# A fused encoder layer on one core: other layouts for two stores in DRAM, row maxima spread evenly over the projection, and the scheduler's detailed model of the chip

## The chip, the core and the metric

The kernel runs on one core of one Trainium2 chip, as one program and one launch. The metric is device time in microseconds (us) from start to end. All arithmetic is float32 in and out; the matrix products use pairs of fp32r numbers, a high half and a low half of each operand, so that one product of two float32 matrices becomes three matmuls (high by high, high by low, low by high).

## What is computed

One layer (DEPTH is 1) on x of 2048 tokens by 1024 features, then a final RMSNorm:

```python
xn = rms_norm(x, mix_norm_g[l])
h = xn @ w_in[l]                                  # 1024 x 2568
q, k, v, f_logit, z = jnp.split(h, [512, 1024, 1536, 1544], axis=-1)
log_f = jax.nn.log_sigmoid(f_logit + b_f[l])
attn = forgetting_attention(q, k, v, log_f)       # 8 heads of 64; logit[t,s] = q.k/8 + c[t] - c[s], s <= t
sgu = spatial_gating(gelu(z), ln_g, ln_b, w_s, b_s)   # z = (zu, zv); zu * (w_s @ layer_norm(zv) + b_s) in chunks of 128
merged = concat([rms_norm(attn, g1), rms_norm(sgu, g2)], axis=-1)
x = x + merged @ w_out[l]                         # 1024 x 1024
xn = rms_norm(x, ffn_norm_g[l])
gate, up = jnp.split(xn @ w_gate_up[l], 2, axis=-1)   # 1024 x 5632
x = x + (silu(gate) * up) @ w_down[l]             # 2816 x 1024
return rms_norm(x, final_norm_g)
```

## The kernel before

**Stage 1, the projections (to about 342 us of the profiled execution).** The tokens stand in four chunks `c` of 512. For each chunk the transposed input is scaled and cut into high and low halves (`xh`, `xl`, four pieces of two k-tiles each, `Chunk.halves`), and TensorE makes q (`which` 0), k (`which` 1) and v. One *unit* of that loop is 24 matmuls into one PSUM tile `mm`: eight k-tiles, three products each. A chunk after the first has 12 units: four for q, four for k, four for v. The halves are also kept in DRAM for a later stage: `Chunk.keep` stores them in `XS`, whose layout is by groups of 128 tokens, [128, 4, 2, 8, 128], so that a later load of one group is one run of 8 KB in each partition, while the store has runs of 128 numbers. v goes to `VD`, laid out by heads, [8, 512, 129].

Between the units stand the row maxima of the chunk before: `max_stream` makes, for each head and block of 128 queries, one matmul into a PSUM tile `mx_ps` and one reduction on VectorE (`one_max`, L357 to L362). `between(n_early, ...)` after each unit takes `n_early` steps of that stream, 3, 6 and 7 in the chunks 1, 2 and 3. Where they stand among the matmuls is settled by the framework's scheduler.

**Stage 2, attention and gating (about 342 to 976 us).** The work is 320 *steps*, each a block of 128 keys against 512 queries of one head. `qk` makes the logits with two matmuls into `mx_ps` (L714, L715), ScalarE takes the exponential (`Pt`, L717) and the high half (`Ph`, L123), VectorE the low half (`Pl`, L126), GpSimd masks blocks on the diagonal (L727), and `pv_of` multiplies with the values, two or three matmuls into `tp` (L747, L749, L752). `mx_ps` has two buffers, which the maxima of stage 2 use too; `Ph` and `Pl` have three. The loop issues the pv of a step two steps behind its qk (DEPTH).

Into these steps the loop mixes the gating branch: `z_proj` makes the z product, 32 tiles of 24 matmuls each (L872, 768 in all), first for zv (tiles of `w` from `wzv`), then for zu. Four tiles make one group of 512 tokens, whose layer norm, gating product (`v_side`, 24 matmuls at L913) or transposes (`u_side`, L940) follow while the next group's product runs. These helpers put their VectorE and ScalarE work behind the newest attention step (`with behind(*newest)`), and share two PSUM buffers `z` with the product. The loop hands out z so that it reaches step 280 (ZEND): 2.4 matmuls a step in the mean. Each z tile needs 1 MB of `XS` (`xz`, two buffers), loaded by GpSimd's queue (L865); the first tile comes from the two halves `wsth` and `wstl`, loaded by SyncE's queue. From about step 281 the output projection (L1127) takes the place of z.

**Stage 3 (to the end).** The rest of the output projection, then the feed-forward part as a seven-product scheme on blocks (L1614, 5544 matmuls).

[...]

Of the kernel before, what the change touches and what calls it, by code (L numbers as in the profile page):

```python
# [16 lines left out]
P = 128  # L17
# [31 lines left out]
HE = [8, 8, 5]  # L49
EB = [1, 12, 12, 10]  # L50

# [34 lines left out]
def trunk(ctx: ExitStack, tc: tile.TileContext, x, x_t, mix_g, w_in, b_f, ln_g, ln_b, w_st, b_st, on_g, w_out,  # L86
# [23 lines left out]
    def behind(*ins):  # L110
# [4 lines left out]
        return s  # L115

    ld = nc.sync.dma_start

    def ldr(o, i):
        return nc.sync.dma_start(f(o), f(i))  # L120
# [27 lines left out]

    XS = [T(dram, [P, 4, 2, KT, P], F32R, f"XS{c}") for c in range(NCH)]
    QH = [[T(dram, [P, CH], F32R, f"QH{p}_{c}") for c in range(NCH)] for p in range(4)]  # L150
    QL = [[T(dram, [P, CH], F32R, f"QL{p}_{c}") for c in range(NCH)] for p in range(4)]
    KH = [[T(dram, [P, CH], F32R, f"KH{p}_{c}") for c in range(NCH)] for p in range(4)]
    KL = [[T(dram, [P, CH], F32R, f"KL{p}_{c}") for c in range(NCH)] for p in range(4)]
    VD = [T(dram, [H, CH, P + 1], F32R, f"VD{c}") for c in range(NCH)]
    FD = [T(dram, [H, CH], F32, f"FD{c}") for c in range(NCH)]
# [85 lines left out]
    class Chunk:  # L241
# [23 lines left out]

        def keep(self, i):
            for a, t in enumerate((self.hi[i], self.lo[i])):
                for m in range(2):
                    s = ldr(XS[self.c][:, :, a, 2 * i + m, :], t[:, m].rearrange("p (t q) -> p t q", t=4))

# [80 lines left out]
    def aug_rows(h, s, r):  # L351
        return AUG.rearrange("(b h) r t -> h r b t", h=H)[h, r, 4 * s : 4 * s + 4, :]

    def one_max(ps, pp, a, j, s, lhs, Dt, mx):
        n = CH if s < j else (a + 1) * P
        pm = T(ps, [P, CH], F32, "mx_ps", **({"bufs": NMX} if ps is ps2_[0] else {}))
        nc.tensor.matmul(pm[:, 0:n], lhs, Dt[0 : lhs.shape[0], 0:n], start=True, stop=True)  # L357
        if s < j:
            nc.vector.tensor_reduce(mx[:, a, s : s + 1], pm, AX.X, ALU.max)  # L359
        else:  # L360
            jk = T(pp, [P, CH], F32, "jk", bufs=1)
            nc.vector.tensor_tensor_reduce(jk[:, 0:n], pm[:, 0:n], dmask[:, CH - n : CH], 1.0, NEG,  # L362
                                           ALU.add, ALU.max, mx[:, a, s : s + 1])
# [62 lines left out]

    def between(n, *done):
        with behind(*done):
            next(gates_, None)
            next(xg, None)  # L430
        for _ in range(n):
            next(early, None)

    def queue(c):
# [14 lines left out]
    def v_close(pm, xc, tt):  # L449
# [7 lines left out]
        b = nc.vector.scalar_tensor_tensor(v[:, :, DH + 1 : P], pmv[:, :, 1:DH], r, f(v[:, :, 1:DH]), ALU.mult, ALU.subtract)  # L457
        s = queue(xc.c if xc.c < NCH - 1 or tt < 2 else 0).dma_start(f(VD[xc.c][:, tt * P : (tt + 1) * P, :].rearrange("h p d -> p h d")), f(v))
        if xc.c == NCH - 1 and tt == 1:
# [58 lines left out]
    for c in range(NCH):  # L518
# [25 lines left out]
        for which, w in ((0, wq), (1, wk)):  # L544
            for pr in range(4):
                pm = T(ps1m, [P, CH], F32, "mm", bufs=4)
                n = 0
                for k in range(KT):
                    lh, ll = w[0][:, k, pr * P : (pr + 1) * P], w[1][:, k, pr * P : (pr + 1) * P]
                    rh, rl = xh[k // 2][:, k % 2, :], xl[k // 2][:, k % 2, :]  # L550
                    for a, b in ((lh, rh), (lh, rl), (ll, rh)):
                        mm = nc.tensor.matmul(pm, a, b, start=n == 0, stop=n == 3 * KT - 1)
                        n += 1
                qh = T(p1, [P, CH], F32R, "qh")
# [22 lines left out]
                if which == (c == 0):  # L577
                    with behind(s):
                        xc.keep(pr)
                if c == which == 0:  # L580
# [5 lines left out]
                if c == NCH - 1 and which and pr:  # L586
                    with behind(a, b):
                        halves_z(pr - 1)
                        if pr < 3:
                            get_z(pr + 1)  # L590
                between(n_early, a, b, mm)
            if c == NCH - 1 and which == 0:
# [58 lines left out]
    def load_keys(h, s, i):  # L651
# [204 lines left out]
    def z_proj(q, w, side, extra, burst):  # L856

        zr = T(p2z, [P, 4, CH], F32, "zr", bufs=2)
        for cc in range(4):
            t = 4 * q + cc  # L860
            if xz0:
                xz = [xz0.pop(0), xz0.pop(0)]
            else:
                xz = T(p2y, [P, 2, KT, P], F32R, "xz")
                nc.gpsimd.dma_start(f(xz.rearrange("p a k t -> p (a k t)")),  # L865
                                    f(XS[q][:, cc].rearrange("p a k t -> p (a k t)")))
                xz = [xz[:, 0], xz[:, 1]]
# [230 lines left out]
    def out_done(t, xt):  # L1098
# [7 lines left out]
        nc.vector.scalar_tensor_tensor(xn, xt, r, E["ffb"], ALU.mult, ALU.mult)
# [68 lines left out]
    with tc.high_priority():  # L1175
# [500 lines left out]
```

## Time and profile before

| | |
|---|---|
| median of 3 runs | 2403.47 us (2403.11 to 2408.91) |
| profiled execution | 2400.57 us, span of its instructions 2398.9 us |
| granted TensorE clock, mean | 0.995 |
| TensorE (PE) busy | 2344.1 us, 98% of the span |
| VectorE (DVE) busy | 1668.5 us, 70% |
| ScalarE (ACT) busy | 1057.5 us, 44% |
| GpSimd (POOL) busy | 636.0 us, 27% |

The table is to be read by stages: shares over the whole span hide that VectorE is at 80 to 85% in stage 2 and TensorE at 100% for most of stage 3. [...] SP stands for SyncE, whose queue issues most of the transfers.

### The profile page before, as it was taken

The page shows a single profiled execution, that of the slowest core. Times are in us where ns is not written, and L with a number is a line of the kernel's source. Part 1 is how long each engine was busy: PE and PEld are TensorE (multiplying, and loading weights), DVE is VectorE, ACT ScalarE, POOL GpSimd, SP SyncE. Part 2 cuts the span into 40 slices and gives each one's busy share as a digit, 9 for nine tenths or more (in the row PEclk, how much of TensorE's full clock was granted, in tenths as well). Part 3 has the DMA queues.
Part 4 walks back from the last instruction along what each step waited for, and adds up shares of the span by engine and source line. Part 5 has one row for each costly group of instructions (what it writes and reads, how often), then busy time and mean ns, then how long its engine had stood idle before and what let it go on. Part 6 is the DMA issues. An engine that isn't in the chain of part 4 may idle for free. (4 is left out here: it accounts for less than half of the span.)

```text
span 2398.9 us, 31422 instructions
## 1 busy us (share of the span) xinstructions
PE 2344.1 (98%) x10582; PEld 1893.2 (79%) x10582; DVE 1668.5 (70%) x2736; ACT 1057.5 (44%) x1770; POOL 636.0 (27%) x704
## 2 busy tenths in 40 slices
PE   9999989999999999999999999999999999999998
PEld 7778767777777767877888888788888878888886
DVE  6658658888887676566656555965556587696888
ACT  5322127777777776444333332433333242332433
POOL 1000011222212232221323232422323244454431
PEclk9999999999999999999999999999999999999999
DMA  9856776555576655665333323433232344555453
GB/s 257 269 155 207 189 197 196 164 156 164 172 214 191 197 167 162 206 209 171 118 89 87 97 71 88 131 98 88 80 96 72 88 135 172 176 193 193 144 202 147
DMA packets 338632, 372.22 MB, mean 155 GB/s; under 512 B 22612, under 2 KB 259860, under 8 KB 332456
## 3 DMA queue, kind: packets, MB, share of 16 engines
q1 hardware_dynamic: 313672, 311.24, 42.9%
q0 software_dynamic: 7472, 43.06, 5.4%
q10 hardware_dynamic: 17328, 15.91, 2.3%
q8 instruction: 85, 1.39, 0.2%
q14 instruction: 75, 0.61, 0.1%
HBM read 249.15 MB, written 120.98 MB: 154 GB/s over the span
## 5 line engine op out<-in xcount | busy, mean ns | idle before, releaser
L123 ACT CAST wh<-raw 128x512 fp32r<-128x512 f32 (+2 forms) x492 | 302.1, 621 | 745.2 <-PE pp L1614 622.9
L126 DVE TENSOR_TENSOR wl<-raw,wh 128x512 fp32r<-128x512 f32 (+2 forms) x496 | 375.5, 767 | 83.8 <-ACT wh L123 83.3
L1614 PE MATMUL pp<-wl,wh 128*128 128x512 f32 x1056 | 325.3, 389 | 1.9 <-ACT u L1414 1.0
L1614 PE MATMUL pp<-wh,wh 128*128 128x512 f32 x1056 | 325.0, 389 | 0.0
L1303 POOL TENSOR_TENSOR raw<-raw 128x512 f32<-128x512 f32 (+1 forms) x124 | 171.1, 1381 | 524.6 <-DMA raw<-in_w_gu_dram 361.1
L126 DVE TENSOR_TENSOR Pl<-Pt,Ph 128x512 fp32r<-128x512 f32 (+1 forms) x320 | 195.9, 617 | 81.0 <-ACT Ph L123 76.3
L1614 PEld LDWEIGHTS pp<-wl,wh 128*128 128x128 f32 x1056 | 198.0, 188 | 43.7 <-ACT u L1414 1.4
L1614 PEld LDWEIGHTS pp<-wh,wh 128*128 128x128 f32 x1056 | 198.2, 188 | 41.1
L717 ACT ACTIVATE Pt<-mx_ps 128x512 f32<-128x512 f32 (+1 forms) x320 | 169.2, 533 | 124.9 <-PE mx_ps L715 119.5
L1614 PE MATMUL pp<-wl,wl 128*128 128x512 f32 x528 | 205.7, 390 | 1.0 <-DVE wl L126 0.9
L1614 PE MATMUL pp<-wh,wl 128*128 128x512 f32 x528 | 205.4, 389 | 0.0
L872 PE MATMUL z<-wh,xz 128*128 128x512 f32 x496 | 188.9, 396 | 0.0
L1303 DVE TENSOR_TENSOR raw<-raw,raw 128x512 f32<-128x512 f32 (+1 forms) x112 | 131.9, 1180 | 78.4 <-POOL raw L1303 74.9
L123 ACT CAST Ph<-Pt 128x512 fp32r<-128x512 f32 (+1 forms) x320 | 176.1, 556 | 20.8 <-PE tp L749 5.9
L359 DVE TENSOR_REDUCE mx<-mx_ps 128x1 f32<-128x512 f32 x192 | 129.8, 682 | 18.7 <-PE mx_ps L357 17.9
L747 PE MATMUL tp<-Ph,V 128*128 128x512 f32 (+1 forms) x320 | 119.1, 372 | 6.1 <-POOL Ph L727 4.5
L357 PE MATMUL mx_ps<-D,A 66*128 66x512 f32 (+2 forms) x320 | 116.7, 380 | 8.2 <-DVE mx L359 4.2
L752 PE MATMUL tp<-Pl,V 128*128 128x512 f32 (+1 forms) x320 | 119.4, 373 | 3.4 <-DVE Pl L126 2.7
L714 PE MATMUL mx_ps<-A,D 74*128 74x512 f32 (+1 forms) x320 | 119.6, 374 | 0.9 <-DMA A<-md 0.6
L715 PE MATMUL mx_ps<-B,C 128*128 128x512 f32 (+1 forms) x320 | 118.1, 369 | 0.0
L1614 PEld LDWEIGHTS pp<-wl,wl 128*128 128x128 f32 x528 | 99.1, 188 | 22.6 <-DVE wl L126 2.1
L1614 PEld LDWEIGHTS pp<-wh,wl 128*128 128x128 f32 x528 | 99.1, 188 | 20.6
(341 smaller groups left out, 5259.8 us busy)
## 6 DMA issues: line engine op xcount, KB each, us to landing
raw<-in_w_gu_dram SPq DMA_DIRECT2D x88, 512.0 KB
xz<-XS POOLq DMA_DIRECT2D x31, 1024.0 KB, 5.6
HD<-hT SPq DMA_DIRECT2D x44, 512.0 KB
D<-KH SPq DMA_DIRECT2D x112, 128.0 KB
XA<-xa SPq DMA_DIRECT2D x27, 512.0 KB
raw<-HD SPq DMA_DIRECT2D x24, 512.0 KB
XA<-xb SPq DMA_DIRECT2D x21, 512.0 KB
xa<-XA SPq DMA_DIRECT2D x20, 512.0 KB
```

The source lines that it names most:

```text
L123: return nc.scalar.copy(o, i) if eng is nc.scalar else eng.tensor_copy(o, i)
L126: return eng.tensor_tensor(o, i, f(h), ALU.subtract)
L357: nc.tensor.matmul(pm[:, 0:n], lhs, Dt[0 : lhs.shape[0], 0:n], start=True, stop=True)
L359: nc.vector.tensor_reduce(mx[:, a, s : s + 1], pm, AX.X, ALU.max)
L714: nc.tensor.matmul(st[:, off:], Dt[:, b * P : (b + 1) * P], A[:, off:], start=True, stop=False)
L715: nc.tensor.matmul(st[:, off:], C[:, b * P : (b + 1) * P], B[:, off:], start=False, stop=True)
L717: nc.scalar.activation(Pt[:, off:], st[:, off:], AF.Exp)
L747: nc.tensor.matmul(pv[:, off:], V[:, 0:P], Ph[:, off:], start=kb == 0, stop=False)
L752: nc.tensor.matmul(pv[:, off:], V[:, 0:P], Pl[:, off:], start=False, stop=kb == 4 * j + 3)
L872: nc.tensor.matmul(pz, xz[a][:, k, :], w[b][:, k, :], start=n == 0, stop=n == 3 * KT - 1)
L1303: (nc.vector if e == "v" else nc.gpsimd).tensor_tensor(o, a, b, op)
L1614: nc.tensor.matmul(pm, a[:, k, :], b[:, k, :], start=on is None and k == 0 and e == 0, stop=k == it.kh - 1 and e == 2, skip_group_check=n ...
```

## The change

Five edits stand together.

1. `XS` is laid out as [128, 2, 8, 512], so that the store of a piece is one run of 4 KB in each partition, and a later load of a token group (`xz`, `wsth`, `wstl`) is 16 runs of 512 B in each partition. The stores move from SyncE's queue to GpSimd's, where the four of a piece (`keep`, 64 in all) become two (32 in all), each with a true wait (`pace`) on the VectorE instruction `b` of its unit. The loads `xz` move from GpSimd's queue to SyncE's.
2. `VD` is laid out by tokens, [512, 8, 129]: a store is one run of 4128 B in each partition, a load still takes runs of 516 B.
3. The steps of `max_stream` are spread over the eight k-tiles of a unit (`maxima`), and the three matmuls of each k-tile are put behind the maximum that was issued three k-tiles ago. `n_early` is 3, 6 and 6 (EB's last entry is 12 instead of 10).
4. In `out_done`, the last two token tiles leave out two pauses of the generator.
5. The context is made with `schedule_with_timeline_sim=True`: the scheduler uses its more detailed model of the chip when it decides what is ready.

```diff
-EB = [1, 12, 12, 10]
+EB = [1, 12, 12, 12]
...
+    def pace(a, b):
+        tc.add_manual_dep(a.ins, b.ins.name, mybir.DependencyInfo(mybir.DependencyClass.Sync, mybir.DependencyReason.DATA),
+                          reason="pace")
...
-    XS = [T(dram, [P, 4, 2, KT, P], F32R, f"XS{c}") for c in range(NCH)]
+    XS = [T(dram, [P, 2, KT, CH], F32R, f"XS{c}") for c in range(NCH)]
-    VD = [T(dram, [H, CH, P + 1], F32R, f"VD{c}") for c in range(NCH)]
+    VD = [T(dram, [CH, H, P + 1], F32R, f"VD{c}") for c in range(NCH)]
...
-        def keep(self, i):
+        def keep(self, i, by):
             for a, t in enumerate((self.hi[i], self.lo[i])):
-                for m in range(2):
-                    s = ldr(XS[self.c][:, :, a, 2 * i + m, :], t[:, m].rearrange("p (t q) -> p t q", t=4))
+                pace(nc.gpsimd.dma_start(f(XS[self.c][:, a, 2 * i : 2 * i + 2, :]), f(t)), by)
...
-    def between(n, *done):
+    def between(*done):
         with behind(*done):
             next(gates_, None)
             next(xg, None)
-        for _ in range(n):
+
+    def maxima(n, k):
+        marks.append(last_mx[-1:])
+        for _ in range((k + 1) * n // KT - k * n // KT):
             next(early, None)
+        return marks[0]
+
+    marks = deque([[], []], maxlen=3)
...
-                    for a, b in ((lh, rh), (lh, rl), (ll, rh)):
-                        mm = nc.tensor.matmul(pm, a, b, start=n == 0, stop=n == 3 * KT - 1)
-                        n += 1
+                    with behind(*maxima(n_early, k)):
+                        for a, b in ((lh, rh), (lh, rl), (ll, rh)):
+                            mm = nc.tensor.matmul(pm, a, b, start=n == 0, stop=n == 3 * KT - 1)
+                            n += 1
...
-                nc.gpsimd.dma_start(f(xz.rearrange("p a k t -> p (a k t)")),
-                                    f(XS[q][:, cc].rearrange("p a k t -> p (a k t)")))
+                ldr(xz.rearrange("p a k t -> p (a k) t"),
+                    XS[q][:, :, :, cc * P : (cc + 1) * P].rearrange("p a k t -> p (a k) t"))
...
         nc.scalar.activation(xn, xt, AF.Square, accum_out=ss)
-        yield
+        if t < NB - 2:
+            yield
         r = rsqrt(pev, ss, 1.0 / D, "r3")
-        yield
+        if t < NB - 2:
+            yield
...
-    with _tile.TileContext(nc) as tc:
+    with _tile.TileContext(nc, schedule_with_timeline_sim=True) as tc:
```

What this moves on the engines is seen at three places.

**TensorE in stage 2, at the start of head 1's second unit** (steps 45 to 49 of 320). `A` and `B` are the queries, `C` and `D` the keys of a step; `mx_ps` from `A`, `D` and `B`, `C` is a qk, `mx_ps` from `D`, `A` a maximum, `tp` a pv, `z` the gating product. Before:

```order
L714 MATMUL mx_ps_4550<-A_4017,D_871_3450 128x512
L715 MATMUL mx_ps_4550<-B_4020,C_866_3445 128x512
L374 MATMUL mx_ps_4559<-ident_63,mh_4394 8x128
L357 MATMUL mx_ps_4565<-D_4247,A_4244 128x512
L747 MATMUL tp_4470<-Ph_4497,V_858_3435 128x512
L749 MATMUL tp_4470<-Ph_4497,V_858_3435 1x512
L752 MATMUL tp_4470<-Pl_4499,V_858_3435 128x512
L714 MATMUL mx_ps_4571<-A_4017,D_867_3446 128x512
L715 MATMUL mx_ps_4571<-B_4020,C_862_3441 128x512
L872 MATMUL z_4507<-wh_2937,xz_4505 128x512
L872 MATMUL z_4507<-wl_2938,xz_4505 128x512
L872 MATMUL z_4507<-wh_2937,xz_4505 128x512
```

Now, at the same two qk (keys `D_871` and `D_867` of the same queries):

```order
L729 MATMUL mx_ps_4518<-A_3985,D_871_3418 128x512
L730 MATMUL mx_ps_4518<-B_3988,C_866_3413 128x512
L767 MATMUL tp_4308<-Pl_4356,V_858_3403 128x256
L729 MATMUL mx_ps_4539<-A_3985,D_867_3414 128x512
L730 MATMUL mx_ps_4539<-B_3988,C_862_3409 128x512
L762 MATMUL tp_4438<-Ph_4444,V_858_3403 128x512
L764 MATMUL tp_4438<-Ph_4444,V_858_3403 1x512
L762 MATMUL tp_4308<-Ph_4420,V_858_3403 128x128
L764 MATMUL tp_4308<-Ph_4420,V_858_3403 1x128
L363 MATMUL mx_ps_4764<-D_4550,A_4212 128x512
L767 MATMUL tp_4308<-Pl_4422,V_858_3403 128x128
L729 MATMUL mx_ps_4562<-A_3985,D_867_3414 128x384
```

The z matmuls have gone from this place, and the pv stand further behind their qk. They now stand earlier: counted over the whole list, the number of z matmuls ahead of qk 25 is 168 instead of 59, and it stays 168 up to qk 70 (before: 174 there). The same is repeated later: the count stands still at 264 (qk 84 to 105), 360 (116 to 138), 456 (152 to 171), 528 (182 to 196), 624 (210 to 229), 720 (246 to 261) and 768 (270 on), while before it never stood still for five steps until all 768 were done at qk 281.

**TensorE at the end of stage 1**, in the v units of chunk 3 (`mm` from `wvh`, `wvl` by `xh`, `xl`; `mx_ps` a maximum). Before:

```order
L357 MATMUL mx_ps_3209<-D_3075,A_3050 128x512
L447 MATMUL mm_3314<-wvh_273,xl_1718 128x512
L447 MATMUL mm_3345<-wvh_273,xh_1711 128x512
L357 MATMUL mx_ps_3212<-D_3075,A_3050 128x512
L447 MATMUL mm_3345<-wvl_274,xh_1711 128x512
L447 MATMUL mm_3345<-wvh_273,xl_1715 128x512
L357 MATMUL mx_ps_3248<-D_3126,A_3050 128x128
L447 MATMUL mm_3345<-wvh_273,xh_1711 128x512
L447 MATMUL mm_3345<-wvl_274,xh_1711 128x512
L357 MATMUL mx_ps_3252<-D_3126,A_3050 128x256
L357 MATMUL mx_ps_3256<-D_3126,A_3050 128x384
```

Now:

```order
L460 MATMUL mm_3210<-wvh_273,xh_1695 128x512
L460 MATMUL mm_3210<-wvl_274,xh_1695 128x512
L460 MATMUL mm_3210<-wvh_273,xl_1699 128x512
L363 MATMUL mx_ps_3190<-D_3062,A_3022 128x512
L460 MATMUL mm_3210<-wvh_273,xh_1695 128x512
L460 MATMUL mm_3210<-wvl_274,xh_1695 128x512
L460 MATMUL mm_3210<-wvh_273,xl_1699 128x512
L363 MATMUL mx_ps_3196<-D_3062,A_3022 128x512
```

A maximum now follows every third or sixth matmul of a unit; before, 66 matmuls without one were followed by a run of 12 maxima, mostly with two matmuls between them and twice with none.

**SyncE's queue at the end of stage 1**, where the first z tile's operands are loaded (`wsth`, `wstl` from `XS`). Before, behind a store of v; now ahead of it:

```order
L120 DMA D_870_3449<-KH_3_46_109 64x512
L458 DMA VD_78_141<-v_3339 128x8x129
L120 DMA wsth_3429<-XS_7_70 128x1024
L120 DMA wstl_3430<-XS_7_70 128x1024
L120 DMA md_2_837_3273<-mr_3271 8x128
```

```order
L125 DMA md_2_818_3182<-mr_3180 8x128
L125 DMA wsth_3397<-XS_7_70 128x8x128
L125 DMA wstl_3398<-XS_7_70 128x8x128
L471 DMA VD_78_141<-v_3307 128x1032
L125 DMA md_2_845_3287<-mr_3285 8x128
```

Both pieces come one place earlier in the queue, and behind fewer key loads, since those of the first attention steps now stand further up.

More of the change, by code (lines that the diff above doesn't have):

```diff
@@ L352, in aug_rows @@
         return AUG.rearrange("(b h) r t -> h r b t", h=H)[h, r, 4 * s : 4 * s + 4, :]
+    last_mx = []
     def one_max(ps, pp, a, j, s, lhs, Dt, mx):
@@ L356, in one_max @@
         pm = T(ps, [P, CH], F32, "mx_ps", **({"bufs": NMX} if ps is ps2_[0] else {}))
-        nc.tensor.matmul(pm[:, 0:n], lhs, Dt[0 : lhs.shape[0], 0:n], start=True, stop=True)
+        last_mx.append(nc.tensor.matmul(pm[:, 0:n], lhs, Dt[0 : lhs.shape[0], 0:n], start=True, stop=True))
         if s < j:
@@ L457, in v_close @@
         b = nc.vector.scalar_tensor_tensor(v[:, :, DH + 1 : P], pmv[:, :, 1:DH], r, f(v[:, :, 1:DH]), ALU.mult, ALU.subtract)
-        s = queue(xc.c if xc.c < NCH - 1 or tt < 2 else 0).dma_start(f(VD[xc.c][:, tt * P : (tt + 1) * P, :].rearrange("h p d -> p h d")), f(v))
+        s = queue(xc.c if xc.c < NCH - 1 or tt < 2 else 0).dma_start(f(VD[xc.c][tt * P : (tt + 1) * P]), f(v))
         if xc.c == NCH - 1 and tt == 1:
@@ L577, in trunk @@
                 if which == (c == 0):
-                    with behind(s):
-                        xc.keep(pr)
+                    xc.keep(pr, b)
                 if c == which == 0:
@@ L590, in trunk @@
                             get_z(pr + 1)
-                between(n_early, a, b, mm)
+                between(a, b, mm)
             if c == NCH - 1 and which == 0:
@@ L597, in trunk @@
             pm = v_open()
-            v_part(pm, xc, tt, range(KT))
+            for k in range(KT):
+                with behind(*maxima(n_early, k)):
+                    v_part(pm, xc, tt, [k])
             a, b, _ = v_close(pm, xc, tt)
@@ L602, in trunk @@
                     halves_z(3)
-            between(n_early, a, b)
+            between(a, b)
             if c == NCH - 1 and tt == 1:
@@ L659, in load_keys @@
         ldr(Dt[64:74].rearrange("r (b t) -> r b t", t=P), aug_rows(h, s, slice(0, 10)))
-        ldr(V, VD[s][h].rearrange("(b p) d -> p b d", p=P))
+        ldr(V, VD[s][:, h].rearrange("(b p) d -> p b d", p=P))
         kd[h, s] = (C, Dt, V)
@@ L1180, in trunk @@
         prep(*units[AHEAD], ab)
-        xz_in = [ldr(xz0[a], XS[0][:, 0, a]) for a in range(2)]
+        xz_in = [ldr(xz0[a], XS[0][:, a, :, 0:P]) for a in range(2)]
     zc = z_consts()
```

## The prediction

> **What bounds the kernel now.** First the page's table of engines, then TensorE's waits, then the stretches of the stages.
>
> ```profile
> PE 2344.1 (98%) x10582; PEld 1893.2 (79%) x10582; DVE 1668.5 (70%) x2736; ACT 1057.5 (44%) x1770; POOL 636.0 (27%) x704
> ```
>
> TensorE (PE) is busy for all but 55 us of the span. Nothing here can gain more than that and a better pace of the matmuls; but a change of order can open new gaps. TensorE's waits, first up to 345 us, then from 345 to 1120 us, then from 1000 to 1200 us:
>
> ```profile
> PE mx_ps L357 <- DVE mx L359: 4.2, 3, 2.5
> PE tp L331 <- DVE v L327: 2.6, 1, 2.6
> PE tp L281 <- DVE rb L276: 1.8, 1, 1.8
> PE mx_ps L470 <- DVE D L467: 1.7, 1, 1.7
> PE mx_ps L357 <- issue: 1.2, 1, 1.2
> PE mx_ps L357 <- DMA D<-KH: 1.2, 1, 1.2
> PE mx_ps L357 <- DVE mx L362: 1.2, 1, 1.2
> ```
>
> ```profile
> PE tp L747 <- POOL Ph L727: 4.5, 8, 1.8
> PE z L872 <- DMA wsth<-XS: 4.3, 1, 4.3
> PE tp L752 <- DVE Pl L126: 2.7, 4, 1.6
> ```
>
> ```profile
> PE tp L1113 <- DVE xb L1106: 3.3, 1, 3.3
> ```
>
> The columns are total us, times, longest. The waits are few and short: 14 us in stage 1, 4.3 us where stage 2 starts, little in attention. Then the stretches: stage 1, the first 310 steps of stage 2 (from the first qk at 341.9 us to the 310th at 950.3), and 100 us of stage 3. Columns: elapsed; busy us of PE, PEld, DVE, ACT, POOL; clock; DMA share; GB/s.
>
> ```profile
> 0.00:341.90 341.90, 327.96 (x1459) 258.94 (x1460) 224.00 (x562) 105.47 (x147) 18.07 (x36) 0.99 0.76 214
> 341.90:950.30 608.40, 590.52 (x2779) 459.17 (x2778) 469.25 (x914) 443.18 (x806) 142.69 (x319) 0.99 0.59 179
> 1200.00:1300.00 100.00, 100.00 (x443) 82.81 (x442) 56.73 (x76) 31.20 (x54) 28.98 (x22) 1.00 0.33 95
> ```
>
> Stage 3 runs at 443 matmuls in 100 us, 0.226 us each: TensorE's best pace for 512 columns. Its list there hardly moves (the same matmuls in the same places but for a few groups), so stage 3 goes in at no change. In stage 2 TensorE is full, but VectorE has 469 and ScalarE 443 of 608 us: they have no room for a stretch in which attention must run much faster than it does now.
>
> **Stage 2: the z matmuls move, the work of the other engines does not.** The z product is what TensorE does while a step passes through exponential, halves and mask. A step's engines, from the groups by form between 397.0 and 466.3 us (behind the bar: busy us, mean ns):
>
> ```profile
> L126 DVE TENSOR_TENSOR Pl<-Pt,Ph 128x512 fp32r<-128x512 f32 x28 | 19.1, 685 | 3.5 <-ACT Ph L123 3.4
> L359 DVE TENSOR_REDUCE mx<-mx_ps 128x1 f32<-128x512 f32 x17 | 11.5, 676 | 0.0
> L737 DVE SCALAR_TENSOR_TENSOR acc<-Ph,V,acc 128x512 fp32r<-128x512 f32 x10 | 7.4, 743 | 0.0
> ```
>
> ```profile
> L123 ACT CAST Ph<-Pt 128x512 fp32r<-128x512 f32 x28 | 17.3, 621 | 1.4 <-ACT Pt L717 0.4 <-ACT Ph L123 0.2
> L717 ACT ACTIVATE Pt<-mx_ps 128x512 f32<-128x512 f32 x28 | 16.5, 597 | 9.2 <-PE mx_ps L715 9.0
> ```
>
> A full step costs ScalarE 1.2 us and VectorE 0.7 us, plus a maximum or a sum, plus the side work of the gating. TensorE's four to five matmuls and a part of a maximum cost 1.1 to 1.2 us. Without z, TensorE outruns them. The new list puts 168 z matmuls ahead of qk 25 and then none up to qk 70, and repeats that with every group of four z tiles. The eight stretches without z (or nearly), by qk: 25 to 64, 82 to 101, 115 to 131, 152 to 162, 182 to 193, 211 to 226, 246 to 258, 270 to 289. The same steps before:
>
> ```profile
> 397.00:466.30 69.30, 68.18 (x321) 53.54 (x320) 60.47 (x114) 54.66 (x96) 17.64 (x37) 1.00 0.59 167
> 500.50:536.30 35.80, 35.28 (x178) 27.25 (x177) 32.45 (x66) 25.68 (x48) 10.54 (x19) 1.00 0.44 130
> 563.90:592.60 28.70, 27.83 (x138) 21.52 (x137) 27.31 (x59) 20.29 (x40) 11.37 (x21) 1.00 0.62 182
> 632.80:647.20 14.40, 14.40 (x66) 11.44 (x65) 13.46 (x22) 10.96 (x21) 1.80 (x2) 1.00 0.59 178
> 689.60:708.10 18.50, 17.97 (x84) 13.88 (x83) 16.37 (x37) 15.68 (x34) 5.90 (x12) 1.00 0.70 212
> 739.50:769.90 30.40, 29.84 (x141) 22.94 (x140) 21.09 (x45) 24.15 (x45) 6.89 (x20) 1.00 0.50 156
> 803.30:827.60 24.30, 24.04 (x115) 18.25 (x114) 15.44 (x31) 20.88 (x40) 7.65 (x19) 1.00 0.55 176
> 848.80:887.10 38.30, 34.97 (x158) 25.00 (x156) 31.46 (x51) 31.91 (x59) 16.05 (x23) 1.00 0.46 139
> ```
>
> The first one worked out. From TensorE's 68.2 us go 103 z matmuls at 0.226 (23.3) and 10 half-wide ones of the gating (1.2); 7 maxima more come in (1.6): 45 us are left. VectorE keeps its 60.5 us and gets 7 reductions at 0.6 (one starts some 0.08 us ahead of the end of the last): 64.7 us. Each pv waits for its `Pl`, and qk runs only some steps ahead of pv, so TensorE cannot leave the stretch sooner than VectorE: 19.5 us idle. The same for the others, with z removed 35, 27, 24, 24, 54, 45 and 27 (in the last also 24 of the output projection, which now start later), and the slower of VectorE and ScalarE: 34.2 against 26.6, 27.9 against 20.6, 14.7 against 9.6, 15.0 against 11.8, 24.2 against 16.3, 20.9 against 12.9, 31.9 against 23.4 (ScalarE in the last three). Together 233 us against 166, 67 us of new idle time.
>
> Corrections. At the end TensorE has three more steps behind it than VectorE (3.5 us, which it had time for), but the first step needs 2 us to reach `Pl`: -1.4 us for each stretch, -11. The waits that stood in these windows before (elapsed less busy, 7 us in all) vanish in the idle time: -7. And VectorE won't run without gaps: where it was fullest (563.9 to 592.6) it was busy for 27.31 of 28.70 us, 95%; 233 us at 95% are 12 us more (bounds 0 and 25, since qk and maxima share two buffers and now wait for each other). Sum for stage 2: 67 - 11 - 7 + 12 = +61. The z matmuls that were pulled forward fill no gap: from the first qk to qk 25 TensorE was busy but for 6 us, most of them the wait for `wsth`.
>
> ```profile
> 341.90:397.00 55.10, 49.15 (x210) 36.38 (x209) 36.00 (x75) 29.24 (x55) 9.14 (x28) 0.94 0.71 190
> ```
>
> **Stage 1 and the passage to stage 2.** The transpose of L331 now stands 9 matmuls later (2.0 us): 2.6 to 0.6. The sums of L281 stand 25 matmuls later: the 1.8 us go. The waits for maxima (4.2 + 1.2 + 1.2 + 1.2) come from maxima in a crowd; evenly spread most should go, but in chunk 2 a unit has 30 matmuls (6.8 us) against 6 reductions, two instructions for q or k and four of the next chunk on VectorE (some 8 us at 0.68), and the matmuls are now pinned behind the maximum: I take half, -4. The first z operands are asked for earlier: half of 4.3, -2. Behind such waits the clock was granted by half for a while:
>
> ```profile
> 334.00:338.00 4.00, 4.00 (x13) 3.16 (x12) 2.42 (x5) 0.00 (x0) 0.00 (x0) 0.63 0.38 102
> 349.60:356.00 6.40, 5.64 (x16) 4.39 (x17) 0.96 (x2) 1.32 (x4) 0.91 (x4) 0.58 0.50 142
> ```
>
> The clock of 0.63 and 0.58 lost 1.5 and 2.7 us there; -3 of these. Sum -13, between +6 (all kept, the pinned chunk waits) and -20.
>
> **The transfers** cost SyncE's queue 64 stores less:
>
> ```profile
> L120 SPq DMA_DIRECT2D XS<-xh x32: 525/609/1561, 68.5 to 290.7; - x32
> ...
> L865 POOL DMA_DIRECT2D xz<-XS x31: 530/557/732, 356.2 to 830.7; - x31
> ...
>   PE z L872: 111.1, 17
> ...
> DMA to landing us min/median/max: 5.0/5.6/8.4
> ```
>
> and give it 31 loads, with the waits for a free `xz` (17 of 111.1 us on GpSimd's queue). Behind them now stand the loads of queries and keys. Two buffers and a z tile of 24 matmuls, stretched by attention to 9 us (7 tiles in 25 steps: 38 us of z and some 27 of attention), cover 0.6 + 5.6 us. I take 0; at worst a tile takes only 5.4 us and each load is 0.7 us late: 31 x 0.7 = +22. GpSimd's 32 stores hide behind its 18 of 342 us. No row shows the shorter runs of the loads or the longer ones of the stores; both move the same bytes, 0.
>
> **The last tiles** (L1106, 3.3 us) lose two pauses: -2.
>
> **The clock.** Three stretches of 4 us around a wait of 1.8 us at 904 us, and that wait:
>
> ```profile
> 900.00:904.00 4.00, 4.00 (x21) 3.21 (x20) 2.04 (x4) 1.28 (x3) 0.60 (x1) 1.00 0.85 249
> 904.00:908.00 4.00, 2.18 (x10) 1.45 (x9) 2.45 (x5) 2.24 (x6) 2.89 (x8) 0.87 1.09 281
> 908.00:912.00 4.00, 4.00 (x18) 3.27 (x16) 1.61 (x3) 1.66 (x3) 0.23 (x1) 0.70 0.39 115
> ```
>
> ```profile
> PE tp L747 <- POOL Ph L727: 1.8, 1, 1.8
> ```
>
> [...] In the new stretches it is busy for 166 of 233 us, 71%, in short pauses; some falls are likely. Inside a stretch they cost nothing until the mean clock is under 0.71; at the end of each, one half-clocked window may reach into the dense part: 8 x 1.7 us at worst, I take +3. [...]
>
> **Sum.** +61 - 13 + 0 - 2 + 3 = +49 on the profiled execution's 2400.57 us: 2450. The median of the runs lies 2.9 us higher: 2453; I say 2450, since the gap term is the least sure.
>
> **Rivals.**
> - Faster: attention carries the surplus across the stretches, so that the z pulled forward is work saved. Then only the gains remain: 2400.6 - 13 - 2 - 7 + 2.9 = 2381. It needs TensorE to run ahead by the whole surplus of a stretch, 8 us in the mean, some 5 steps beyond the usual lag; three buffers of `Ph` and `Pl` and two of `mx_ps` speak against it. Chance 0.07.
> - The stretches cost half (VectorE's side work slips into the dense parts): 2450 - 30 = 2420. The lists put that work in the same steps as before. 0.12.
> - Stage 1 gains nothing, as pinned maxima wait in chunk 2: 2450 + 13 = 2463, with the worst 2469. 0.14.
> - Loads of `xz` hold up SyncE's queue: 2450 + 22 = 2472. 0.09.
> - The clock stays at half through the stretches: TensorE needs 332 us there instead of 233, +99: 2549 at worst, with half of that 2500. A TensorE busy all the time gets its clock back, as after 908 us. 0.05.
> - The forecast, 2430 to 2470: 0.53.
>
> **The range.** From 2412 (the second rival with a gap term of 4 us) to 2492 (the forecast with 25 instead of 12 us for gaps, SyncE's 22 and a part of the clock's) it leaves out the faster case and most of the clock's. About 0.3% (7 us) is what a measurement can tell from no change: faster 0.08 (the first rival and a tail of the second), same 0.04, slower 0.88.
>
> **What would show it.** After the change TensorE's busy share in stage 2 swings: near full up to qk 25, then about 70% of full for over 60 us with VectorE above 90%, and so on in eight waves; its waits name `Pl` (or the mask behind it) and the reductions of `mx_ps`, some 70 us in all, where it was under 10. The first qk should come about 10 us sooner. Stage 3 should last the same to 2 us. Wrong it is if VectorE is far from full in those stretches, if TensorE waits for transfers instead, or if stage 2 lasts under 630 us from the first qk to the 310th.

## Result: 2441.5 us, 1.5% slower, and the profile after

The changed kernel takes 2441.52 us (median of 4 runs, 2440.11 to 2442.23) against 2403.48: ratio 1.0152, 95% interval 1.0135 to 1.0170. The profiled execution has a span of 2438.4 us, 39.5 more than before. The stages in the traces of before and after (a qk is taken at its second matmul, stage 3 from the start of its first to the start of its last matmul):

| us | before | after | difference | forecast |
|---|---|---|---|---|
| to the first qk | 341.9 | 334.7 | -7.2 | about -10 |
| first to 310th qk | 608.4 | 654.0 | +45.6 | +61, most of +3 for the clock, and some -3 of the stage 1 term |
| 310th qk to stage 3 | 166.3 | 168.0 | +1.7 | 0 |
| stage 3 | 1270.5 | 1272.2 | +1.7 | 0, to 2 us |
| behind the last matmul of stage 3 | 11.7 | 9.6 | -2.1 | -2 |

The engines of the page, as before with TensorE first:

```profile
PE 2369.7 (97%) x10582; PEld 1907.2 (78%) x10582; DVE 1660.7 (68%) x2736; ACT 1048.1 (43%) x1770; POOL 631.7 (26%) x705
```

The same number of matmuls is busy 26 us longer: the clock was at half for 71.0 us of the span, before for 24.1 (in both traces a matmul of 512 columns that waits for nothing starts 0.227 us after the one before it at full clock, 0.427 at half; medians). The stretches, with the columns of before (elapsed; busy PE, PEld, DVE, ACT, POOL with their instructions; clock; DMA share; GB/s): stage 1; stage 2; qk 1 to 25; the eight bare stretches (steps with no z matmul, or a few at the edge) in order; 100 us of stage 3.

```profile
0.00:334.70 334.70, 323.68 (x1450) 257.76 (x1451) 224.25 (x564) 105.40 (x147) 35.11 (x68) 0.99 0.66 221
334.70:988.70 654.00, 617.01 (x2791) 470.42 (x2790) 467.58 (x911) 431.51 (x805) 120.89 (x288) 0.96 0.59 165
334.70:407.90 73.20, 71.73 (x331) 57.40 (x330) 36.72 (x72) 32.77 (x62) 7.45 (x25) 1.00 0.69 192
407.90:473.60 65.70, 53.92 (x205) 35.17 (x204) 59.55 (x119) 49.61 (x91) 11.76 (x28) 0.89 0.46 126
519.60:546.60 27.00, 24.82 (x121) 17.86 (x120) 26.90 (x52) 20.95 (x43) 6.86 (x16) 1.00 0.50 133
585.40:606.80 21.40, 19.91 (x94) 14.01 (x92) 21.38 (x46) 16.55 (x35) 9.40 (x17) 1.00 0.68 174
657.60:668.70 11.10, 10.48 (x45) 7.12 (x43) 11.10 (x23) 9.51 (x19) 0.00 (x0) 1.00 0.96 228
715.70:730.60 14.90, 13.31 (x52) 8.79 (x52) 12.60 (x28) 14.10 (x33) 3.49 (x9) 0.89 0.79 205
777.50:798.70 21.20, 17.50 (x67) 12.19 (x66) 15.87 (x33) 20.26 (x40) 2.26 (x8) 0.84 0.38 98
847.40:866.10 18.70, 14.82 (x57) 10.93 (x56) 10.38 (x18) 17.34 (x33) 4.38 (x11) 0.73 0.34 97
892.60:923.90 31.30, 27.61 (x113) 18.85 (x111) 26.57 (x45) 27.51 (x52) 13.56 (x23) 0.95 0.52 138
1200.00:1300.00 100.00, 100.00 (x443) 82.81 (x442) 58.71 (x81) 33.02 (x56) 32.02 (x23) 1.00 0.33 92
```

The reader is to see three things. The waves are there: TensorE does 331 matmuls in 73 us up to qk 25, then 205 in 66 us. In the second to fourth bare stretch VectorE is busy all the time (26.90 of 27.00, 21.38 of 21.40, 11.10 of 11.10), in the fifth to seventh ScalarE nearly so (14.10 of 14.90, 20.26 of 21.20, 17.34 of 18.70), and in the first VectorE for 91%; in the eighth ScalarE is the fuller with 88%. Stage 3 has the same 443 matmuls in 100 us. The eight stretches last 211.2 us (259.8 before, when z stood in them), the rest of the 310 steps 442.8 (348.6).

The bare stretches are shorter than the same steps were, and yet the loss is in them. To see it, take from each the time that its matmuls need at stage 3's pace (0.226 us for 512 columns, narrower ones in proportion). In the eight stretches the matmuls needed 231.3 us before and need 139.8 now, so the time beyond it went from 28 to 71 us, +43. In the rest of the 310 steps they needed 310.7 us and need 404.7, and the time beyond it is 38 us in both: 8.5 us less up to qk 25 and as much more further on.

TensorE's waits in stage 2 (total us, times, longest):

```profile
PE mx_ps L729 <- ACT Pt L732: 14.0, 24, 2.2
PE tp L762 <- ACT Ph L128: 5.0, 3, 2.4
PE tp L762 <- POOL Ph L742: 4.4, 6, 1.4
PE tp L767 <- DVE Pl L131: 4.2, 6, 1.1
PE mx_ps L363 <- DMA D<-AUG: 2.7, 2, 1.7
```

A qk waits for the exponential that has still to read its `mx_ps`. It is attention that holds TensorE up for most of its 37 us of idle time; transfers have 2.7 us, for a key tile of the maxima.

In stage 1 one long wait is new. The wait, and six pieces of 3.4 us around it:

```profile
PE mx_ps L363 <- DMA D<-AUG: 6.2, 1, 6.2
```

```profile
302.35:305.75 3.40, 3.40 (x18) 2.84 (x17) 2.17 (x7) 0.40 (x1) 0.73 (x1) 1.00 0.91 238
305.75:309.17 3.42, 2.14 (x10) 1.41 (x8) 3.31 (x9) 1.17 (x2) 0.01 (x1) 1.00 0.98 232
309.17:312.58 3.41, 0.27 (x1) 0.08 (x1) 0.29 (x2) 0.00 (x0) 0.71 (x1) 1.00 0.86 269
312.58:315.99 3.41, 0.28 (x1) 0.31 (x2) 0.00 (x0) 0.00 (x0) 0.00 (x0) 0.50 0.67 177
315.99:319.41 3.42, 3.42 (x9) 2.65 (x9) 1.29 (x2) 0.00 (x0) 0.00 (x0) 0.50 0.52 183
319.41:322.82 3.41, 3.41 (x17) 2.78 (x16) 2.15 (x5) 1.62 (x2) 0.00 (x0) 1.00 0.52 154
```

TensorE stands still from 309.5 to 315.7 us, as a maximum waits for the last rows of its key tile `D`, and then does 9 matmuls in 3.4 us where it did 18. On SyncE's queue that load (issued at 312.3) stands behind the block of early loads for the first attention units. Since the matmuls of a unit are now put behind the maxima, they can't pass it.

### The profile page after: what moved, and what is told of

It is laid out like the page before. It is cut to its first block, busy times and chain, and to the rows that moved or that the text cites. A ratio compares the mean times of both kernels' runs of the same rounds, so it can differ in the third digit from the quotient of the medians.

```text
span 2438.4 us, 31521 instructions
## 1 busy us (share of the span) xinstructions
PE 2369.7 (97%) x10582; PEld 1907.2 (78%) x10582; DVE 1660.7 (68%) x2736; ACT 1048.1 (43%) x1770; POOL 631.7 (26%) x705
## 4 chain that ended last, share of the span: by engine, by line
PE 69%; DVE 7%; issue 2%; ACT 2%; DMA 1%; POOL 0%; SPq 0%; POOLq 0%; ACTq 0%; DVEq 0%
PE pp L1631 48%; PE z L887 5%; PE pp L1144 4%; PE oz L1144 2%; PE tp L767 2%; PE tp L762 2%; PE mx_ps L729 2%; PE mx_ps L730 2%; DVE wl L131 1%; DVE Pl L131 1%; PE tp L764 1%; PE mx_ps L363 1%; ACT Pt L732 0%; ACT Ph L128 0%; DVE acc L752 0%
## 5 line engine op out<-in xcount | busy, mean ns | idle before, releaser
L131 DVE TENSOR_TENSOR wl<-raw,wh 128x512 fp32r<-128x512 f32 (+2 forms) x496 | 398.6, 813 | 84.9 <-ACT wh L128 84.8
L1631 PE MATMUL pp<-wh,wh 128*128 128x512 f32 x1056 | 325.2, 389 | 0.0
L1320 POOL TENSOR_TENSOR raw<-raw 128x512 f32<-128x512 f32 (+1 forms) x124 | 179.7, 1451 | 508.9 <-DMA raw<-in_w_gu_dram 352.7
L887 PE MATMUL z<-wh,xz 128*128 128x512 f32 x496 | 170.1, 396 | 0.1
L742 POOL TENSOR_SCALAR_AFFINE_SELECT Ph<-Ph 128x128 fp32r<-128x128 f32 x128 | 50.6, 396 | 382.2 <-DVE Pl L131 254.3
L729 PE MATMUL mx_ps<-A,D 74*128 74x512 f32 (+1 forms) x320 | 126.1, 395 | 14.1 <-ACT Pt L732 14.0
L363 PE MATMUL mx_ps<-D,A 66*128 66x512 f32 (+2 forms) x320 | 120.8, 382 | 12.5 <-DMA D<-AUG 8.8
L762 PE MATMUL tp<-Ph,V 128*128 128x512 f32 (+2 forms) x320 | 121.9, 383 | 9.5 <-ACT Ph L128 5.0
L767 PE MATMUL tp<-Pl,V 128*128 128x512 f32 (+1 forms) x320 | 124.5, 390 | 5.2 <-DVE Pl L131 4.2
L1320 DVE TENSOR_TENSOR raw<-raw,raw 128x512 f32<-128x512 f32 (+1 forms) x112 | 95.7, 855 | 39.1 <-POOL raw L1320 35.6
L1631 PEld LDWEIGHTS pp<-wl,wl 128*128 128x128 f32 x528 | 99.1, 188 | 20.5
```

Of the source, the lines that this page charges most:

```text
L131: return eng.tensor_tensor(o, i, f(h), ALU.subtract)
L363: last_mx.append(nc.tensor.matmul(pm[:, 0:n], lhs, Dt[0 : lhs.shape[0], 0:n], start=True, stop=True))
L729: nc.tensor.matmul(st[:, off:], Dt[:, b * P : (b + 1) * P], A[:, off:], start=True, stop=False)
L762: nc.tensor.matmul(pv[:, off:], V[:, 0:P], Ph[:, off:], start=kb == 0, stop=False)
L767: nc.tensor.matmul(pv[:, off:], V[:, 0:P], Pl[:, off:], start=False, stop=kb == 4 * j + 3)
L887: nc.tensor.matmul(pz, xz[a][:, k, :], w[b][:, k, :], start=n == 0, stop=n == 3 * KT - 1)
```

## Experiments

Stage times in us; ratio to runs of the kernel before on the same chip, with its 95% interval. "Edits" are numbered as in the change. Half-clocked time is what the trace's clock records hold between the first and the 310th qk; before the change it is 10.2 us, after it 47.8.

| kernel | first qk | qk 1 to 310 | half clock there | median | ratio |
|---|---|---|---|---|---|
| edit 5 alone | 387.8 | 656.1 | 58.6 | 2497.27 | 1.0389 (1.0376 to 1.0402) |
| edits 1 to 4 | 331.4 | 607.0 | 3.4 | 2386.49 | 0.9925 (0.9913 to 0.9936) |
| all, z held back | 336.1 | 619.3 | 13.7 | 2406.23 | 1.0010 (1.0001 to 1.0019) |
| all, TensorE filled | 335.0 | 665.5 | 47.8 | 2450.76 | 1.0194 (1.0180 to 1.0207) |
| all, `Pl` twice, bare steps | 334.9 | 751.6 | 167.3 | 2538.69 | 1.0562 (1.0549 to 1.0576) |
| all, `Pl` twice, dense steps | 335.8 | 678.9 | 64.9 | 2467.35 | 1.0274 (1.0258 to 1.0289) |
| all, unpinned | 381.6 | 665.7 | 70.3 | 2497.75 | 1.0395 (1.0381 to 1.0408) |
| edits 1 to 4, block later | 329.5 | 605.6 | 0 | 2388.36 | 0.9937 (0.9921 to 0.9954) |
| all, keys on GpSimd | 333.2 | 663.7 | 58.0 | 2452.17 | 1.0199 (1.0183 to 1.0216) |
| edits 1 to 4, keys on GpSimd | 322.7 | 608.6 | 6.8 | 2378.63 | 0.9887 (0.9874 to 0.9901) |
| edits 1 and 2 | 331.1 | 605.3 | 6.8 | 2384.47 | 0.9911 (0.9895 to 0.9926) |
| edits 3 and 4 | 343.9 | 610.2 | 3.4 | 2405.54 | 1.0003 (0.9991 to 1.0015) |

### The scheduler's model alone, and everything but it

```diff
-    with _tile.TileContext(nc) as tc:
+    with _tile.TileContext(nc, schedule_with_timeline_sim=True) as tc:
```

On the kernel before:

> The kernel before with the scheduler's detailed model and nothing else. Its list has the same standstills of z as the changed kernel (168 z matmuls ahead of qk 25, none up to qk 70, and so on). Theory A (the standstills set the loss): stage 2 from the first to the 310th qk lasts 645 to 660 us as after the change (654.0), against 608.4 before; time 2435 to 2450. Rival B (the loss comes from the loads of xz on SyncE's queue and the short runs of XS): nothing of that is here, so stage 2 lasts 605 to 615 us and the time is 2400 to 2410.

Taken out of the changed kernel:

> The changed kernel with the old model of the scheduler: both layouts, the moved queues, the even maxima, the two pauses. Theory A: stage 2 605 to 612 us from the first to the 310th qk, first qk at 325 to 335 us (the 6.2 us wait for a key row of the maxima at 309 us should not be there, since the row's load stands ahead of the block of early loads in this list); time 2385 to 2398. Rival B: stage 2 at 640 us or more, time 2430 or more.

Of the five edits, stage 2 goes by this one: 656.1 us with it alone, 607.0 without it, where the kernels before and after have 608.4 and 654.0. The total of the first run was missed by some 50 us, because stage 1 became 46 us longer. Its first stage, and TensorE's waits in it:

```profile
0.00:387.80 387.80, 359.25 (x1472) 271.89 (x1472) 228.91 (x564) 106.25 (x148) 17.97 (x36) 0.91 0.67 193
```

```profile
PE mx_ps L357 <- DVE mx L359: 8.2, 15, 2.4
PE mx_ps L357 <- DVE mx L362: 7.5, 12, 2.4
PE mx_ps L357 <- DMA D<-AUG: 4.5, 1, 4.5
```

Where nothing holds the maxima they come in a crowd, each waiting for the reduction on VectorE before it, and the clock was at half for 71 us of this stage. On top of edits 1 to 4 the flag costs 2441.5 - 2386.5 = 55 us, alone it costs 94: the parts don't add.

### The pins taken away

```diff
-                    with behind(*maxima(n_early, k)):
+                    maxima(n_early, k)
+                    with behind():
```

and the same in the v units.

> The changed kernel without the three pins: the maxima are issued evenly over the k-tiles as before, but the matmuls of a k-tile are no longer put behind the maximum of three k-tiles ago. Theory A (the detailed model clumps the maxima as soon as nothing holds them, as the flag alone did in the kernel before, where the first qk came at 387.8 us): the first qk comes at 360 to 390 us instead of 334.7, 2467 to 2497. Rival B (the even issue alone keeps them apart, the pins do nothing): first qk at 330 to 340, 2436 to 2447.

The first qk comes at 381.6 us, as theory A said; the total lies just above its range, as stage 2 became 11.7 us longer too, though the edit is in stage 1. An even issue in the code is undone by the detailed model; the order edges of edit 3 keep it. TensorE's waits for the reductions are back, and a wait for a key tile is there without the pins:

```profile
PE mx_ps L363 <- DVE mx L365: 7.7, 18, 1.7
PE mx_ps L363 <- DVE mx L368: 6.6, 10, 2.9
PE mx_ps L363 <- DMA D<-KH: 3.9, 1, 3.9
```

### z held back

```diff
+                with behind(*newest_qk):
                     for a, b in ((0, 0), (0, 1), (1, 0)):
                         nc.tensor.matmul(pz, xz[a][:, k, :], w[b][:, k, :], ...)
```

`newest_qk` is the second matmul of the latest qk, so that z can't be pulled forward past it.

> The changed kernel, detailed model and all, with one more edge in the order: the z matmuls of a k-tile stand behind the qk that was newest when the code issued them, so z is spread as before (54 instead of 168 ahead of qk 25, 174 ahead of qk 70). Theory A: the loss of stage 2 goes, 605 to 618 us from the first to the 310th qk, half clock in stage 2 under 15 us; time 2393 to 2410, the 6.2 us wait of stage 1 still there. Rival B (queues and layout) or C (the model's other moves in stage 2): 2430 to 2445 still.

Stage 2 (the row below) gets 34.7 of the 45.6 us back, with the detailed model still in use; the expected 605 to 618 us were just missed. The half-clocked time falls to 13.7 us. The time beyond the matmuls' need in the steps of the eight stretches is back at 29 us (28 before, 71 with the whole change); of the 10.9 us that stay, 7 are in the other steps and 2.5 are more matmul work between the first and the 310th qk. So the bare stretches are the cause of the loss, by whatever way they cost time.

```profile
336.10:955.40 619.30, 592.42 (x2791) 464.74 (x2790) 464.05 (x910) 429.60 (x804) 130.67 (x288) 0.99 0.63 174
```

### What sets the pace in the bare stretches: TensorE filled, VectorE loaded

One more matmul in each of the 141 bare steps, overwritten by the real ones:

```diff
+        for _ in range(EXTRA if any(lo <= n < hi for lo, hi in BARE) else 0):
+            nc.tensor.matmul(st[:, off:], Dt[:, b * P : (b + 1) * P], A[:, off:], start=True, stop=True)
```

> The changed kernel with the first matmul of a qk issued twice in the 141 steps of the eight stretches without z (the second overwrites the first, the result is the same): 29 to 32 us more of TensorE work, all of it in the stretches. Theory A1 (TensorE idles there because VectorE or ScalarE sets the pace): within 6 us of the changed kernel, 2436 to 2448. A2 (much of the loss is the half clock that the idle time brings): 2420 to 2434, with far less than the 48 us of half clock in stage 2. Against A (TensorE's own work sets the pace there after all): 2465 to 2475.

141 matmuls of at most 0.226 us are some 30 us; they cost 9.3 (2450.8 against 2441.5), just above A1's range. TensorE had time for two thirds of them or more: other edits that add no work to stage 2 moved it by 10 to 12 us under this flag (the pins taken away, and the keys on GpSimd below), so the 9.3 us can't be told from a new order of the list. The half-clocked time stayed at 47.8 us, so filling it this way did not hold the clock up.

The counterpart, the low half made twice in 141 steps:

```diff
         i_l = lo_of(nc.vector, Pl[:, off:], Pt[:, off:], Ph[:, off:])
+        if any(lo <= steps.index((h, j, kb)) < hi for lo, hi in TWICE):
+            i_l = lo_of(nc.vector, Pl[:, off:], Pt[:, off:], Ph[:, off:])
```

> The changed kernel, with the low half Pl made twice (the second instruction writes the same numbers) in the 141 steps of the eight stretches that hold no z matmul. One such instruction takes 0.58 us in the mean (186.8 us for 320), so VectorE gets 82 us more there, against some 27 us that it is idle in them (211.2 us long, 184 busy). Theory A (VectorE and ScalarE set the pace of the bare stretches, TensorE has time over): all of it that doesn't fit lengthens them, +50 to +80 us, 2490 to 2522. Rival B (the stretches are long because TensorE itself runs at half clock or waits on latency from step to step): VectorE has time to spare wherever it isn't named in a wait, and the same number of extra instructions costs the same in the dense parts: +10 to +35 in both.

> The counterpart: Pl made twice in 141 steps of the stretches that are full of z matmuls (the first seven and five steps of the eighth). VectorE is busy there for 206 of 328 us (first stretch 36.7 of 73.2, the others 25 to 37 of 39 to 51), so 82 us more still fit. Theory A: 0 to +15 us, 2442 to 2457. Rival B (latency from step to step): +10 to +35, as much as in the bare stretches.

In the bare steps the extra work costs 97 us, in the dense ones 26. Both are above theory A's ranges, but the difference is A's: by B they would cost the same. In the first of the two, VectorE's busy time in the eight stretches rises by 81 us (184.3 to 265.2) and their length by 79 (211.2 to 290.2), one for one. Its first two bare stretches (65.7 and 27.0 us in the changed kernel):

```profile
407.60:492.80 85.20, 67.82 (x226) 44.41 (x224) 82.61 (x162) 49.56 (x89) 14.66 (x28) 0.76 0.37 102
541.80:587.90 46.10, 38.66 (x154) 27.09 (x154) 42.88 (x90) 23.64 (x47) 11.96 (x23) 0.81 0.29 89
```

VectorE is busy for 97% and 93% of them, and TensorE, left with more idle time, runs at 0.76 and 0.81 of its clock. In the second kernel the eight dense stretches grow by 6 us and the bare ones by 20.5, whose VectorE time rises by 17.5 (184.3 to 201.8): so a part of the work slides from the dense stretches into the bare ones. That sliding A had not foreseen. ScalarE's part, in the fifth to seventh bare stretch of the changed kernel, rests on its busy share alone; no run loads it.

### Edits 1 and 2 alone, edits 3 and 4 alone

The kernel before with the two layouts and the moved queues:

> The kernel before with edits 1 and 2 alone: the two layouts, the stores to XS on GpSimd's queue, the loads xz on SyncE's. Theory A (the 17 us that edits 1 to 4 gain come mostly from the maxima of edit 3, since stage 1 is where they were gained): the first qk comes at 337 to 342 us, stage 2 is the same to 2 us, 2394 to 2403. Rival B (64 stores less on SyncE's queue are the gain): first qk at 331 to 335, 2385 to 2393. A loss in stage 2 over 3 us would show that the loads xz on SyncE's queue do cost something.

The kernel before with the maxima spread and pinned and the pauses left out:

> The kernel before with edits 3 and 4 alone: the maxima spread evenly and the matmuls pinned behind them, the pauses left out; layouts, queues and scheduler as before. Theory A (the gain of stage 1 is the shorter queue of SyncE, and the pins by themselves make TensorE wait for a key row that is late there: three of the last rows stand behind the block of early loads): first qk at 340 to 352 us, 2402 to 2418. Rival B (the even spread itself removes the waits for maxima, 4 to 8 us): first qk at 333 to 338, 2393 to 2400.

Rival B of the first (its total 0.5 us under the range) and theory A of the second hold. The layouts and the stores on GpSimd's queue alone gain 20.5 us on the kernel before, edits 3 and 4 alone nothing. With the layouts alone the waits for reductions of maxima, 4.2 + 1.2 us before, are down to 0.7, though their issue is not spread. In the profiled execution, the slowest of the five, 10.8 of the 12.5 us by which its span is shorter lie ahead of the first qk. With the pins alone TensorE waits for a key tile behind the block of early loads, as after the whole change; there the first qk comes 2 us later than before. The loads `xz`, now on SyncE's queue, bring two waits in stage 2, 5.1 us, where before `wsth` had 4.3, but stage 2 is no longer for it: 605.3 us against 608.4. Stage 1 of the first, a wait of it in stage 2, and stage 1 of the second with its longest wait:

```profile
0.00:331.10 331.10, 325.81 (x1454) 257.88 (x1455) 223.00 (x562) 105.55 (x147) 35.19 (x68) 0.99 0.66 222
```

```profile
PE z L875 <- DMA xz<-XS: 5.1, 2, 4.3
```

```profile
0.00:343.90 343.90, 322.93 (x1424) 254.67 (x1425) 225.37 (x557) 104.96 (x146) 18.04 (x36) 0.98 0.76 214
```

```profile
PE mx_ps L364 <- DMA D<-AUG: 6.9, 1, 6.9
```

That the gain comes from SyncE's queue being shorter by 64 stores of 0.6 us is argued from these two runs and not shown by itself: edit 1 also moves where the transfers' bytes lie.

### The wait for the key tile

First the block of early loads one store later, without the flag:

```diff
-        with behind(k_low[1]):
+        with behind(k_low[2]):
```

> Edits 1 to 4 without the detailed model, and the block of early loads for stage 2 put behind the third k store of the last chunk instead of the second, so that the key row of the last maxima stands ahead of it on SyncE's queue. Theory A (that block holds up the row: a wait of 4.1 us at 320 us and 10.2 us of half clock behind it, some 5 us lost): both go, 2374 to 2381 against 2386.5. Rival B (the row is late for another reason, or the block's loads now come too late for the first steps of stage 2): 2384 to 2395.

It did not settle it: 2388.4 us (rival B's range), with runs from 2381.7 to 2393.4. The wait of edits 1 to 4, the row here,

```profile
PE mx_ps L363 <- DMA D<-KH: 4.1, 1, 4.1
```

went, but the block now stood ahead of the next key tile, whose last rows were asked for only at 322.8 us, and TensorE stood until 325.2 (the profile names no releaser):

```profile
PE mx_ps L363 <- issue: 5.7, 1, 5.7
```

Then the loads of these key tiles on another queue, in the last chunk alone:

```diff
-                ldr(Dt[0:64], KH[pr][s][o : o + DH])
+                row = (lambda o, i: nc.gpsimd.dma_start(f(o), f(i))) if j == 2 and ps is not ps2_[0] else ldr
+                row(Dt[0:64], KH[pr][s][o : o + DH])
```

(and the second load of `D` alike). With the flag, and without it:

> The changed kernel, with the loads of the key tiles D of the last chunk's early maxima on GpSimd's queue instead of SyncE's, where the block of early loads for stage 2 stands ahead of the last of them. Theory A (that block is what TensorE waits for at 309 us, and the half clock behind it is its consequence): the wait of 6.2 us and the 6.8 us of half clock at 312.6 us go, the first qk comes at 324 to 329 us instead of 334.7, the whole 2430 to 2436 against 2441.5. Rival B (GpSimd's queue is as late, since it stands behind stores that wait, or the row itself is written late): a wait of the same size, 2438 to 2446.

> The same edit on edits 1 to 4 without the detailed model. Theory A: the wait of 4.1 us at 320 us and the 10.2 us of half clock go, the first qk comes at 322 to 327 us instead of 331.4, the whole 2376 to 2382 against 2386.5. Rival B: 2384 to 2390.

Without the flag theory A holds: no such wait is left, the first qk comes at 322.7 us, and the whole takes 2378.6 us, ratio 0.9887, the lowest median here, though its interval still touches that of edits 1 and 2. With the flag A fails. The query rows of the same maxima (`A`), which were left on SyncE's queue, are as late:

```profile
PE mx_ps L363 <- DMA A<-CR: 5.2, 1, 5.2
```

and stage 2 takes 10 us more (663.7), though the edit is in stage 1. The pins taken away did the same (665.7). That the detailed model makes another order for stage 2 at any such edit is the likely reason, not shown step by step.

## Why the prediction was right, and where its terms were not

The direction, the place and the mechanism hold: the bare stretches are where the time goes, VectorE and ScalarE set the pace there, stage 3 and the passage move by under 2 us each. The size holds too, 2450 forecast and 2441.5 measured, but in part by luck: the main term was 18 us too large and the gain of stage 1 some 3 too large, and edits 1 to 4 came to their forecast sum by another way than the one given.

**The bare stretches: right in kind, 18 us too large.** +61 was forecast, and +43 is what these steps lose beyond the need of their matmuls. The step that failed is "the lists put that work in the same steps as before". VectorE's work in all eight fell from 218 to 184 us and ScalarE's from 204 to 176: a part of it now lies in the dense stretches, so the second rival's mechanism took a part of its share. The second to fourth and the sixth and seventh stretch were forecast at 121.9 us and took 99.4. For the first, fifth and eighth the forecast (64.7, 15.0, 31.9 us) was met (65.7, 14.9, 31.3), in the first and the eighth by errors that cancel: VectorE in the first had 5 us less work and 6 us of gaps, ScalarE in the eighth 4 us less and 4 us of gaps. The +12 for VectorE's gaps was not needed in the second to fourth stretch (busy 99 to 100%). Of the reason given for that term one part was wrong, and the description of the kernel with it: `mx_ps` of qk and `mx_ps` of the maxima of stage 2 stand in different pools with two buffers each and don't share them.

**The signs.** VectorE was to be above 90% in all eight waves. It was in the first four; in the last four it was at 85, 75, 56 and 85%, and ScalarE at 95, 96, 93 and 88%. The waits were to name `Pl` and the reductions; they name the exponential first (14.0 us) and `Pl` with 4.2. In the bare stretches the chain runs through ScalarE, which in turn waits for `Pl` in the first one. And the idle time is 37 us where about 70 were forecast: TensorE's records cover 86% of the bare stretches and not 70%, though its matmuls need only 66% of them at full pace (a record of 512 columns lasts 0.39 us at full clock, where starts come 0.227 us apart).

**The clock: +3, and open.** Half-clocked time in stage 2 went from 10.2 to 47.8 us, 38.2 of it in the bare stretches. If TensorE had had to run all that time, 37.6 us more at half clock would have cost some 18, an estimate from the 0.427 us between starts there against 0.227. Most lies where VectorE or ScalarE sets the pace, and there the prediction's argument (no cost until the mean clock is below TensorE's share of the work) stands. What it did cost wasn't isolated: no run shows the term of +3, which was the author's estimate, and in its place the runs show these half-clocked times alone. The clock fell eight times in stage 2, where TensorE's longest gap was 2.4 us.

**Stage 1: some -10 forecast ahead of the first qk, -7.2 measured, and for other reasons.** Its old waits did go (L331, L281, most reductions), but the pinned matmuls met a key tile that was late, 6.2 us, and lost half its clock for 6.8 us behind that. The prediction looked for the pins' cost in chunk 2's reductions; it stood on SyncE's queue in chunk 3. And the gain was credited to the maxima and to moved instructions, while the runs give it to edits 1 and 2.

**The transfers: 0 forecast.** This is the worst-sized term. Edits 1 and 2 alone are worth -20.5 us on the kernel before, edits 3 and 4 alone nothing. The prediction saw 64 stores leave SyncE's queue and priced only what came in their place. Its sum for edits 1 to 4 came out right by luck, -15 forecast (-13 and -2) and -17 measured, with the gain booked to the wrong ones. For the flag it had +64 (+61 and +3), and 55 us were measured on top of the others.

**The last tiles: -2, met by chance.** The end behind stage 3 takes 10.0 us with edit 5 alone and 12.6 with edits 1 to 4, so the flag's order brought it, not the two pauses.

## What to carry to other kernels

A scheduler that pulls independent matmuls forward empties the stretches they came from; price a stretch by the slowest of the engines that remain, from the profile of before, and expect their side work to move as well. Under the detailed model, work spread by hand stayed spread only where order edges held it, and whatever is pinned inherits the wait of the thing it is pinned behind: look at what stands ahead of that load on its queue. Price each queue for what leaves it too (here the likely source of the gain, not isolated), and take a bundle of edits apart before keeping it: here one line cost 55 us and hid a gain of 17.

## What the runs showed of the hardware

The length of a gap alone does not tell where the clock fell. In the changed kernel's stage 2 it fell to half at 718.8 and at 903.1 us with no gap of TensorE over 0.91 us in the 3.41 us before, and it stayed full behind a gap of 1.65 us that ended at 532.1. Nine traces (before, after, and the first seven kernels of the table) were cut into windows of 3.41 us, the steps in which their clock records change (the half-clocked records of the changed kernel last 3.41, 6.83 or 10.24 us, but for the one at the end). The fill of a window is the time that the matmuls starting in it need, counted as 0.226 us for 512 columns where the clock is full and as twice that where it is at half (measured there: 0.427 us, 1.9 times). At full clock, 80 of the 81 windows under 0.35 were followed by a half-clocked one, so were 30 of the 105 between 0.35 and 0.55, and none of the 6034 above 0.55. At half clock, the next window was full again after 85 of the 89 that were filled to 0.95 or more, after 15 of 30 between 0.85 and 0.95, and after 1 of 98 below. These are counts, and where a matmul over an edge is put shifts them by a few.

So in these nine traces a window filled to between 0.55 and 0.85 kept the clock it had, with one exception at most. An estimate from these counts: work that needs 70% of the time at full clock keeps it there, and at half clock, where it needs 140% as counted here (132% at 0.427 us), it fills its windows and gets the full clock back. In the changed kernel's stage 2 the half-clocked periods last 3.4 to 10.2 us. Work that needs about half of the time did worse: with `Pl` made twice, the first bare stretch needs 42.7 of its 85.2 us at full pace, and TensorE is at half clock for 41 us of it.

Four pieces of the changed kernel:

```profile
435.55:438.96 3.41, 3.41 (x19) 2.60 (x18) 3.08 (x6) 3.10 (x6) 0.54 (x2) 1.00 0.49 133
438.96:442.37 3.41, 1.71 (x8) 1.00 (x7) 2.98 (x7) 3.36 (x5) 1.74 (x5) 0.99 0.70 205
442.37:449.20 6.83, 5.47 (x16) 4.40 (x17) 5.53 (x12) 5.26 (x10) 0.54 (x2) 0.51 0.21 62
449.20:452.60 3.40, 3.40 (x19) 2.43 (x17) 3.40 (x9) 2.50 (x7) 0.00 (x0) 1.00 0.24 77
```

Eight matmuls in one window (1.71 us busy; the longest pause that reaches into it is 2.2 us) are followed by two windows at half clock, in which 16 matmuls keep TensorE busy for 80% of the time.
